# Attention's output projection: weight splits with a lead of 10, lo parts on POOL, chunks at 0.75 a half step

## The chip, the cores and the metric

The kernel runs on one core of a Trainium2 chip. A core has five engines that run side by side and wait for one another through semaphores: PE (TensorE, matrix products), DVE (VectorE) and ACT (ScalarE) for elementwise work and reductions, POOL (GpSimd) for elementwise work, and SP (SyncE), which here issues all DMAs. Each engine takes its instructions strictly in the order in which they stand. The metric is the device time of one launch in microseconds (us); less is better.

## What is computed

Two layers of a diffusion backbone over 256 latent tokens and 256 context tokens of width 1024. Layer 0 is a half-step SwiGLU FFN, a 2-D neighbourhood attention with 16 heads, and a second FFN; layer 1 has a short convolution in attention's place. Every sub-layer ends in a residual and a layer norm. All is float32. The part around the change, cut from the reference:

```python
bias = rpb[:, dy_idx[None, None, :, None], dx_b].reshape(N_HEADS, ncb, NA_QC, nk)
s_win = jnp.einsum('bjqhd,bjkhd->bhjqk', q_r, k_blk).astype(jnp.float32) * scale
s_win = jnp.where(mask, s_win + bias.astype(jnp.float32)[None], -jnp.inf)
s_ctx = jnp.einsum('bjqhd,bchd->bhjqc', q_r, k_c).astype(jnp.float32) * scale
p = jax.nn.softmax(jnp.concatenate([s_win, s_ctx], axis=-1), axis=-1).astype(v.dtype)
...
y_lat = jnp.moveaxis(o, 0, 1).reshape(B, S, D) @ w_out
...
x = post_norm_update(x, y_lat, m[:, 5], 1.0, ln_g[i, 1], ln_b[i, 1])
```

## The kernel before

Each float32 product is made of three products of a rounded type: an operand is split into a hi part (ACT copies it to the rounded type) and a lo part (the rest, a subtraction on DVE), and PE adds hi x hi, hi x lo and lo x hi (`mmu`, lines 156 to 159). For weights, `wunit` does it: it loads a raw block of 128x1024 by DMA (tile wor for the output projection), makes the hi part woh in two ACT instructions of 128x512 and the lo part wol in two DVE instructions of 128x512. Pools hold four raw blocks and five hi and lo blocks each; a load waits until the lo part of the block four units before has been made.

PE's order is the program's order, as it is written (`manual_schedule`). On the other engines a planner orders the instructions by priority; `high_priority(offset=n)` puts what stands inside it earlier by n places. The weight splits have an offset of 40 from the first FFN on, softmax's steps 40 and 70.

Attention has 32 half steps, one for a head and 128 queries. At each even step `scores` makes the scores S of a pair of heads (six matmuls), DVE adds the bias tile and takes the maximum, ACT takes the exponential and scales it (tile pr). The bias is loaded by four DMAs a pair, and POOL adds the window's mask to it (line 730). Two half steps later `probs_T` transposes the probabilities (PT, four matmuls) and splits them into pT hi (ACT) and lo (DVE); a step after that, for a head whose two query halves are there, `values` makes the eight matmuls o, whose halves are added (osum) and split (oT). The banks in PSUM are few: two for transposes, three for S and one half of the projection, three for o and the other half.

Between these steps stands a filler: at first the key, value and query projections, in the last eight half steps and behind them the output projection, `last_filler`. It goes by chunks: one chunk is one step of `out_gemm`, one weight unit for one bank, six matmuls of 128x512. There are eight units (pairs of K tiles for two halves of the columns) and sixteen chunks. The list `rate` says how many chunks stand at each half step; nine of them may stand among the softmax steps, the other seven behind them, since they need the last heads. Pairs of scores are numbered 0 to 15, chunks 1 to 16, units 1 to 8 in order of use.

Of the kernel before, what the change touches and what calls it, by code (L numbers as in the profile page):

```python
# [9 lines left out]
F32 = mybir.dt.float32  # L10
F32R = mybir.dt.float32r
AF = mybir.ActivationFunctionType
ALU = mybir.AluOpType
# [17 lines left out]
WB = (4, 5, 5)  # L31
PB = {"mm": 3, "at": 3, "tp": 2}
W_EARLY = 40
ADA_LATE = 20
LN_EARLY = 60
LEAD = 5
# [5 lines left out]
R0 = 2.4  # L42
R1 = 2.9
R2 = 1.9
R3 = 1.0
LN_LAG = (5, 5)
LT_LAG = (5, 5)
F0_LAG = (5, 5, 6, 7)
# [16 lines left out]
def backbone_kernel(  # L65
# [6 lines left out]
    nc = tc.nc  # L72
# [9 lines left out]

    uid = [0]
    w_early = [0]
    ext = [1, 0]
    ada_late = [0]

    def nm(s):
        uid[0] += 1
        return f"{s}_{uid[0]}"  # L90

    def act(dt=F32, s="a"):
        return ap.tile([P, 512], dt, tag="act", name=nm(s))
# [51 lines left out]
    def set_background(gen, rate):  # L145
        background[:] = [gen, rate, 0.0]
# [15 lines left out]
    def wunit(srcs, kn, s):  # L162

        raw = wp.tile([P, UN], F32, tag="wr", bufs=WB[0], name=nm(s + "r"))
        ext[1] += 1
        if ext[0] and ext[1] % (5 + ext[0]) in (E0 if ext[0] == 1 else E2):
            hi = hp.tile([P, UN], F32R, tag="whx", bufs=ext[0], name=nm(s + "h"))
            lo = hp.tile([P, UN], F32R, tag="wlx", bufs=ext[0], name=nm(s + "l"))
        else:
            hi = wp.tile([P, UN], F32R, tag="wh", bufs=WB[1], name=nm(s + "h"))  # L170
            lo = wp.tile([P, UN], F32R, tag="wl", bufs=WB[2], name=nm(s + "l"))
        rv, hv, lv = (t[:, :kn * 512].rearrange("p (a b) -> p a b", a=kn) for t in (raw, hi, lo))
        with tc.high_priority(offset=w_early[0]):
            for src, c in srcs:
                sync.dma_start(rv[:, :, c:c + src.shape[2]], src)
            m = kn * 512
            for a in range(0, m, m // W_HI):
                nc.scalar.activation(hi[:, a:a + m // W_HI], raw[:, a:a + m // W_HI], AF.Copy)  # L178
            for a in range(0, m, m // W_LO):
                b = a + m // W_LO  # L180
                nc.vector.tensor_tensor(out=lo[:, a:b], in0=raw[:, a:b], in1=hi[:, a:b].bitcast(F32), op=ALU.subtract)  # L181
        return hv, lv

    def wrows(w, r0, n, c0, s):
        src = w[r0:r0 + n * P, c0:c0 + 512].rearrange("(k p) n -> p k n", p=P)
        return wunit([(src, 0)], n, s)

    def wpair(w, u, c0, c1, s):
        if c1 == c0 + 256:
            return wrows(w, u * UK * P, UK, c0, s)  # L190
        src = w[u * UK * P:(u + 1) * UK * P, :].rearrange("(k p) n -> p k n", p=P)
        return wunit([(src[:, :, c0:c0 + 256], 0), (src[:, :, c1:c1 + 256], 256)], UK, s)
# [79 lines left out]
    def stream(*groups):  # L272
        for g in groups:
            yield from ada(g)
# [54 lines left out]
    def modulated(z, mv, rs, GB, lag):  # L329

        for h in range(2):
            nc.vector.tensor_scalar(z[h], z[h], mv[:, 0:1], rs, op0=ALU.subtract, op1=ALU.mult)

        def rest():
            G, B = GB.get()
            res = []
            for h in range(2):
                ps = tpb("hT")
                for k in range(4):
                    nc.tensor.transpose(ps[:, k * P:(k + 1) * P], z[h][:, k * P:(k + 1) * P], ident)  # L340
                t = sp.tile([P, 512], F32, tag="s2", bufs=S2, name=nm("h"))
                with tc.high_priority(offset=LN_EARLY):
                    hi, lo = act(F32R, "hTh"), act(F32R, "hTl")
                    for k in range(4):
                        s, c = slice(k * P, (k + 1) * P), slice(4 * h + k, 4 * h + k + 1)
                        nc.scalar.activation(t[:, s], ps[:, s], AF.Identity, bias=B[:, c], scale=G[:, c])
                    split(t, hi, lo)
                res.append((hi, lo))
            return res

        return Late(lag, rest)
# [29 lines left out]
    def run(gen):  # L381
        for _ in gen:
            pass
# [37 lines left out]
    def order_late(nu):  # L421

        e = nu - 1
        banks = ((0, 0), (0, 1), (1, 0))
        o = [(t, n, u) for t, n in banks for u in range(e - 1)]
        o += [(t, n, u) for u in (e - 1, e) for t, n in banks]
        return o + [(1, 1, u) for u in range(nu)]
# [47 lines left out]
    def start_step(k0, n):  # L475
# [31 lines left out]
        def mod(k, px):  # L507
            t = sp.tile([P, 512], F32, tag="s2", bufs=S2, name=nm("h"))
            hi, lo = act(F32R, "h0h"), act(F32R, "h0l")
            with tc.high_priority(offset=W_EARLY):  # L510
                for v in range(2):
# [62 lines left out]
    sync.dma_start(rope, rope_tab.rearrange("(t p) a b -> p t a b", p=P))  # L574
    w_early[0] = W_EARLY
    set_background(stream([(0, 2, 0), (0, 2, 1)], [(0, 3, 0), (0, 3, 1)], [(0, 4, 0), (0, 4, 1)],
# [5 lines left out]
    for fh, (p0, p1) in enumerate(parts):  # L582
# [16 lines left out]
        if fh == 0:  # L599
# [5 lines left out]
            background[1] = 0.4  # L605
            ada_late[0] = ADA_LATE

# [29 lines left out]
    def sub_end(w, lhs, nk, l, i, gm, wgt, nxt, s, order):  # L637


        gate = mod_rows(l, gm, "gate")  # L640
        lnr = None if nxt else ln_rows(l, i)
        GB = fold_cols(nxt[0], 0, nxt[1], (l, i)) if nxt else None
        st, hTs = {}, [None, None]

        def evac(t, n, bank, *c):
            if n == 0:
                st[t] = stat_tile(2 if nxt or t == 0 else 3)
            part = nxt is None and t == n == 1
            cs = slice(*(c or (0, 512)))
            residual(bank, xt[t][n][:, cs], gate[n][:, cs], wgt, None if c else ALPHA,  # L650
                     None if part and not c else st[t][:, n + (c[0] // 256 if c else 0)])
            if n == 1 and (not part or c and c[1] == 512):
                mv, rs = finish_stats(st[t])
                if nxt:
                    hTs[t] = modulated(xt[t], mv, rs, GB, (LN_LAG if nk > KC else LT_LAG)[t])
                else:
                    for h in range(2):
                        nc.vector.scalar_tensor_tensor(out=xt[t][h], in0=xt[t][h], scalar=mv[:, 0:1], in1=lnr[0][h],
                                                       op0=ALU.subtract, op1=ALU.mult)
                    for h in range(2):  # L660
                        nc.vector.scalar_tensor_tensor(out=xt[t][h], in0=xt[t][h], scalar=rs, in1=lnr[1][h],
                                                       op0=ALU.mult, op1=ALU.add)
                        sync.dma_start(out[0, t * P:(t + 1) * P, h * 512:(h + 1) * 512], xt[t][h])

        return out_gemm(w, lhs, nk, order, evac, s), hTs, (lambda: new_x(l, i))

    def lhs_T(tl):
        def f(k, t):
            s = (k % 2) * 256 + t * P
            g = tl[k // 2]  # L670
            hi, lo = g.get() if isinstance(g, Late) else g
            return hi[:, s:s + P], lo[:, s:s + P]
        return f
# [197 lines left out]
    def filler():  # L871
        yield from kv_quarter(1, KV)
        yield from kv_quarter(2, KV)
        yield from q_half(1, Q)
        yield from kv_quarter(3, KV)

    def last_filler():
        with tc.issue_after(bias_dma[-1].ins):
            for t in range(2):
                for h in range(2):  # L880
                    xt[t][h] = act(F32, "x")
                    sync.dma_start(xt[t][h], xscr[t * P:(t + 1) * P, h * 512:(h + 1) * 512])
            gen, nh, lt = sub_end(na_w_out[0], lhs_T(oT), KC, 0, 1, 5, 1.0, (0, 6), "wo", order_late(KU))
        box.extend([nh, lt])
        yield from gen

    box = []
    fill = filler()
    rate = [R0] * 8 + [R1] * 8 + [R2] * 8 + [R3] * 12
    credit = 0.0  # L890
    steps = [(h + i, qt) for h in range(0, NH, 2) for qt in range(2) for i in range(2)]
    prs = {}
# [37 lines left out]
                values(steps[j][0])  # L930
    run(fill)
    run(fin)
    phase.__exit__(None, None, None)
    hTs, later = box
    phase = tc.tile_pool(name="ph2", bufs=1)
# [127 lines left out]
```

## Time and profile before

| | us |
|---|---|
| median of 3 runs | 1286.15 |
| lowest, highest | 1283.31, 1291.49 |
| the profiled execution's own time | 1289.17 |
| its span | 1287.4 |

The second half of attention, on which the change works, runs from about 543 to 602 us of the span: S of pairs 10 to 15, the last transposes of the keys kT, chunks 1 to 16. Before it PE works on the projections, behind it follows the second FFN of layer 0. A matmul of 128x512 starts 0.23 us after the one before it, and its own length of 0.39 us overlaps the next. In the timeline's rows, the brackets hold the idle time of the engine ahead of an instruction and what ended it. In the views of waits, the numbers are the total, the count and the longest.

### The profile page before, as it was taken

The page shows a single profiled execution, that of the slowest core. Times are in us where ns is not written, and L with a number is a line of the kernel's source. Part 1 is how long each engine was busy: PE and PEld are TensorE (multiplying, and loading weights), DVE is VectorE, ACT ScalarE, POOL GpSimd, SP SyncE. Part 2 cuts the span into 40 slices and gives each one's busy share as a digit, 9 for nine tenths or more (in the row PEclk, how much of TensorE's full clock was granted, in tenths as well). Part 3 has the DMA queues.
Part 4 walks back from the last instruction along what each step waited for, and adds up shares of the span by engine and source line. Part 5 has one row for each costly group of instructions (what it writes and reads, how often), then busy time and mean ns, then how long its engine had stood idle before and what let it go on. Part 6 is the DMA issues. An engine that isn't in the chain of part 4 may idle for free.

```text
span 1287.4 us, 17193 instructions
## 1 busy us (share of the span) xinstructions
PE 1257.7 (98%) x5890; PEld 1007.0 (78%) x5890; DVE 955.1 (74%) x1683; ACT 591.2 (46%) x1148; POOL 42.0 (3%) x71
## 2 busy tenths in 40 slices
PE   7999999999999999988999999999999999999997
PEld 4787778788778877766887787887787877788886
DVE  3699877485658777788998787757778788855545
ACT  2432132413236456686555435654435645655431
POOL 0000000000001111110000000000000000000000
PEclk9999999999999999999999999999999999999999
DMA  9977569484622744464999887666887764666641
GB/s 284 299 231 243 181 193 297 131 297 146 198 78 76 215 91 92 90 147 149 305 331 328 295 294 262 215 215 225 289 287 241 215 211 147 210 217 185 231 155 51
DMA packets 202712, 268.59 MB, mean 209 GB/s; under 512 B 30026, under 2 KB 149298, under 8 KB 202624
## 3 DMA queue, kind: packets, MB, share of 16 engines
q1 hardware_dynamic: 202624, 267.49, 65.9%
q8 instruction: 46, 0.75, 0.2%
q14 instruction: 42, 0.34, 0.1%
HBM read 265.27 MB, written 2.17 MB: 208 GB/s over the span
## 4 chain that ended last, share of the span: by engine, by line
PE 78%; DVE 8%; DMA 8%; ACT 3%; issue 2%; SPq 1%; POOL 0%; DVEq 0%; ACTq 0%
PE w L156 13%; PE w L157 13%; PE w L159 13%; PE f L541 6%; PE f L542 6%; PE f L543 6%; DMA ar<-in_ada_w_dram 5%; DMA w1r<-in_ffn_w_in_dram 2%; PE wkv L156 2%; PE wkv L157 2%; PE wkv L159 2%; PE wc L156 2%; PE wc L157 2%; PE wc L159 2%; DVE w1l L181 2%
## 5 line engine op out<-in xcount | busy, mean ns | idle before, releaser
L178 ACT ACTIVATE w1h<-w1r 128x512 fp32r<-128x512 f32 x352 | 203.3, 626 | 185.0 <-PE w L159 75.4
L181 DVE TENSOR_TENSOR w1l<-w1r,w1h 128x512 fp32r<-128x512 f32 x352 | 227.6, 684 | 66.5 <-ACT w1h L178 64.3
L156 PE MATMUL w<-w1h,hTh 128*128 128x512 f32 x528 | 211.6, 401 | 3.8 <-ACT hTh L105 3.7
L247 DVE SCALAR_TENSOR_TENSOR acc<-ar,cst,acc 128x512 f32<-128x512 f32 x266 | 187.2, 745 | 34.8 <-DMA ar<-in_ada_w_dram 34.8
L157 PE MATMUL w<-w1l,hTh 128*128 128x512 f32 x528 | 207.7, 393 | 0.0
L156 PE MATMUL w<-w2h,gh 128*128 128x512 f32 (+1 forms) x446 | 175.4, 394 | 0.0
L157 PE MATMUL w<-w2l,gh 128*128 128x512 f32 (+1 forms) x446 | 173.7, 390 | 0.3 <-DVE w2l L181 0.3
L178 ACT ACTIVATE w2h<-w2r 128x512 fp32r<-128x512 f32 x176 | 101.5, 624 | 140.9 <-PE w L159 131.6
L159 PE MATMUL w<-w1h,hTl 128*128 128x512 f32 x528 | 163.9, 392 | 0.6 <-DVE hTl L106 0.6
L181 DVE TENSOR_TENSOR w2l<-w2r,w2h 128x512 fp32r<-128x512 f32 x176 | 114.0, 686 | 43.5 <-ACT w2h L178 42.3
L541 PE MATMUL f<-h0h,w1h 128*128 128x512 f32 x352 | 139.8, 397 | 0.4 <-ACT w1h L178 0.4
L542 PE MATMUL f<-h0h,w1l 128*128 128x512 f32 x352 | 138.4, 393 | 0.0
L543 PE MATMUL f<-h0l,w1h 128*128 128x512 f32 x352 | 138.3, 393 | 0.0
L159 PE MATMUL w<-w2h,gl 128*128 128x512 f32 (+1 forms) x446 | 136.3, 387 | 0.0
L156 PEld LDWEIGHTS w<-w1h,hTh 128*128 128x128 f32 x528 | 99.5, 188 | 28.2 <-ACT hTh L105 5.5
L159 PEld LDWEIGHTS w<-w1h,hTl 128*128 128x128 f32 x528 | 99.5, 189 | 24.1 <-DVE hTl L106 1.4
L157 PEld LDWEIGHTS w<-w1l,hTh 128*128 128x128 f32 x528 | 99.6, 189 | 20.4 <-DVE w1l L181 0.3
L156 PEld LDWEIGHTS w<-w2h,gh 128*128 128x128 f32 x446 | 83.7, 188 | 21.7 <-issue 1.7
L157 PEld LDWEIGHTS w<-w2l,gh 128*128 128x128 f32 x446 | 83.8, 188 | 18.6 <-DVE w2l L181 1.3
L159 PEld LDWEIGHTS w<-w2h,gl 128*128 128x128 f32 x446 | 83.3, 188 | 18.7
L541 PEld LDWEIGHTS f<-h0h,w1h 128*128 128x128 f32 x352 | 66.6, 189 | 18.4 <-issue 3.7
L543 PEld LDWEIGHTS f<-h0l,w1h 128*128 128x128 f32 x352 | 66.5, 189 | 14.7 <-DVE h0l L519 0.3
(178 smaller groups left out, 1702.5 us busy)
## 6 DMA issues: line engine op xcount, KB each, us to landing
w1r<-in_ffn_w_in_dram SPq DMA_DIRECT2D x352, 256.0 KB
ar<-in_ada_w_dram SPq DMA_DIRECT2D x128, 512.0 KB
w2r<-in_ffn_w_out_dram SPq DMA_DIRECT2D x88, 512.0 KB
ar<-in_ada_w_dram SPq DMA_DIRECT2D x32, 256.0 KB
wkvr<-in_na_w_qkv_dram SPq DMA_DIRECT2D x32, 256.0 KB
wcr<-in_sc_w_in_dram SPq DMA_DIRECT2D x32, 256.0 KB
wqr<-in_na_w_qkv_dram SPq DMA_DIRECT2D x8, 512.0 KB
bias<-in_na_rpb_dram SPq DMA_DIRECT2D x64, 64.0 KB
```

What stands on the lines that cost most here:

```text
L156: nc.tensor.matmul(ps, lh, rh, start=first and i == 0, stop=False)
L157: nc.tensor.matmul(ps, lh, rl, start=False, stop=False)
L159: nc.tensor.matmul(ps, ll, rh, start=False, stop=last and i == n - 1)
L178: nc.scalar.activation(hi[:, a:a + m // W_HI], raw[:, a:a + m // W_HI], AF.Copy)
L181: nc.vector.tensor_tensor(out=lo[:, a:b], in0=raw[:, a:b], in1=hi[:, a:b].bitcast(F32), op=ALU.subtract)
L247: nc.vector.scalar_tensor_tensor(out=a, in0=src, scalar=sc, in1=a, op0=ALU.mult, op1=ALU.add)
L541: nc.tensor.matmul(ps, lh, hT0[k][0], start=(k == 0), stop=False)
L542: nc.tensor.matmul(ps, ll, hT0[k][0], start=False, stop=False)
L543: nc.tensor.matmul(ps, lh, hT0[k][1], start=False, stop=(k == KC - 1))
```

## The change

While the output projection of attention is made (`calm`), a unit is split with an offset of 10 instead of 40. Its hi part is one ACT instruction of 128x1024, and its lo parts are two POOL instructions of 128x512 instead of two on DVE. Its load keeps the offset of 40. Through `rate`, half steps 24 to 31 take 0.75 chunks each instead of 1.0; the last four keep 1.0. No arithmetic changes.

```diff
+CALM = 10
+R4 = 0.75
...
         with tc.high_priority(offset=w_early[0]):
             for src, c in srcs:
                 sync.dma_start(rv[:, :, c:c + src.shape[2]], src)
-            m = kn * 512
+        m = kn * 512
+        if calm[0]:
+            with tc.high_priority(offset=CALM):
+                nc.scalar.activation(hi[:, :m], raw[:, :m], AF.Copy)
+                for a in range(0, m, 512):
+                    nc.gpsimd.tensor_tensor(out=lo[:, a:a + 512], in0=raw[:, a:a + 512],
+                                            in1=hi[:, a:a + 512].bitcast(F32), op=ALU.subtract)
+            return hv, lv
+        with tc.high_priority(offset=w_early[0]):
             for a in range(0, m, m // W_HI):
...
     def last_filler():
+        calm[0] = True
...
-    rate = [R0] * 8 + [R1] * 8 + [R2] * 8 + [R3] * 12
+    rate = [R0] * 8 + [R1] * 8 + [R2] * 8 + [R4] * 8 + [R3] * 4
...
     run(fin)
+    calm[0] = False
```

On PE, behind the scores of pair 13 (S_939; PT is a transpose of the probabilities, o a product with the values, wo a chunk), there stood before:

```order
L814 MATMUL S_939_5169<-kTh_907_5053,qTl_821_4643 128x512
L156 MATMUL wo_949_5206<-woh_947_5199,oT_724_4188 128x512
L157 MATMUL wo_949_5206<-wol_948_5200,oT_724_4188 128x512
L159 MATMUL wo_949_5206<-woh_947_5199,oT_725_4189 128x512 x2
L836 MATMUL PT_952_5215<-ident_75,pr_915_5077 128x128 x4
L848 MATMUL o_953_5222<-pT_903_5039,v_708_4110 128x256
```

There stands now:

```order
L825 MATMUL S_939_5167<-kTh_907_5053,qTl_821_4643 128x512
L847 MATMUL PT_948_5198<-ident_75,pr_915_5077 128x128 x4
L859 MATMUL o_949_5205<-pT_903_5039,v_708_4110 128x256
L860 MATMUL o_949_5205<-pT_904_5040,v_757_4365 128x256
L159 MATMUL wo_953_5225<-woh_951_5219,oT_724_4188 128x512
L160 MATMUL wo_953_5225<-wol_952_5220,oT_724_4188 128x512
```

The chunk no longer stands between S and PT but behind o; behind the scores of pair 15 it is the same.

On PE, at the end of softmax, from the last chunk before the last transposes to chunk 10 (wo on woh_1002), there stood before:

```order
L159 MATMUL wo_968_5288<-woh_982_5357,oT_902_5036 128x512 x2
L836 MATMUL PT_996_5423<-ident_75,pr_976_5338 128x128 x4
L836 MATMUL PT_997_5430<-ident_75,pr_978_5345 128x128 x4
L848 MATMUL o_998_5437<-pT_984_5370,v_830_4682 128x256
L848 MATMUL o_1000_5449<-pT_993_5408,v_830_4682 128x256
L156 MATMUL wo_930_5121<-woh_1002_5463,oT_988_5390 128x512
```

There stands now:

```order
L162 MATMUL wo_930_5120<-woh_991_5386,oT_902_5036 128x512 x2
L847 MATMUL PT_993_5398<-ident_75,pr_976_5328 128x128 x4
L162 MATMUL wo_953_5225<-woh_995_5406,oT_902_5036 128x512 x2
L847 MATMUL PT_997_5418<-ident_75,pr_978_5335 128x128 x4
L859 MATMUL o_998_5425<-pT_979_5339,v_830_4682 128x256
L162 MATMUL wo_969_5291<-woh_991_5386,oT_902_5036 128x512 x2
L859 MATMUL o_1000_5443<-pT_985_5369,v_830_4682 128x256
L159 MATMUL wo_930_5120<-woh_1002_5457,oT_983_5359 128x512
```

Of each chunk and each o one row is shown. One chunk has come between the last two transposes PT, and one between the last two o.

On POOL, in the middle of the second half (bias_881 and 882 are pair 11's bias, 895 and 896 pair 12's, 918 pair 13's), there stood before:

```order
L730 TENSOR_TENSOR bias_881_4940<-bias_881_4940,wmask_99 128x256
L730 TENSOR_TENSOR bias_882_4944<-bias_882_4944,wmask_99 128x256
L730 TENSOR_TENSOR bias_895_5007<-bias_895_5007,wmask_99 128x256
L730 TENSOR_TENSOR bias_896_5011<-bias_896_5011,wmask_99 128x256
L730 TENSOR_TENSOR bias_918_5088<-bias_918_5088,wmask_99 128x256
```

There stands now:

```order
L741 TENSOR_TENSOR bias_881_4940<-bias_881_4940,wmask_99 128x256
L184 TENSOR_TENSOR wol_934_5136<-wor_932_5134,woh_933_5135 128x512
L741 TENSOR_TENSOR bias_882_4944<-bias_882_4944,wmask_99 128x256
L184 TENSOR_TENSOR wol_952_5220<-wor_950_5218,woh_951_5219 128x512 x2
L184 TENSOR_TENSOR wol_967_5273<-wor_965_5271,woh_966_5272 128x512 x2
L741 TENSOR_TENSOR bias_895_5007<-bias_895_5007,wmask_99 128x256
L184 TENSOR_TENSOR wol_992_5387<-wor_990_5385,woh_991_5386 128x512 x2
L741 TENSOR_TENSOR bias_896_5011<-bias_896_5011,wmask_99 128x256
L741 TENSOR_TENSOR bias_918_5088<-bias_918_5088,wmask_99 128x256
```

The second lo part of wol_934 stands between bias_882 and wol_952 as well. The lo parts of units 2 to 5 now stand among the biases of pairs 11 and 12; those of unit 1 stand ahead of pair 9's, those of units 6 to 8 behind pair 15's.

On ACT the hi part of unit 5 now stands ahead of both scalings of pair 10, where the first half of it stood behind both; the hi parts of units 6 and 7 stand ahead of the exponentials or scalings of pair 15, and that of unit 8 stands between the last two osum copies. On SP the load of unit 5 is now issued ahead of pair 9's bias and that of unit 8 ahead of pair 13's, where they stood behind pair 9's and behind the loads of the layer norm's rows. In the FFNs some weight splits and sums of the adaLN rows (w1l, w2l, acc) change places on DVE, and so do a few of their loads on SP.

More of the change, by code (lines that the diff above doesn't have):

```diff
@@ L84, in backbone_kernel @@
     w_early = [0]
+    calm = [False]
     ext = [1, 0]
```

## The prediction

> **What bounds the kernel now.** I read the page first: its busy times and the chain of waits.
>
> ```profile
> PE 1257.7 (98%) x5890; PEld 1007.0 (78%) x5890; DVE 955.1 (74%) x1683; ACT 591.2 (46%) x1148; POOL 42.0 (3%) x71
> PE 78%; DVE 8%; DMA 8%; ACT 3%; issue 2%; SPq 1%; POOL 0%; DVEq 0%; ACTq 0%
> ```
>
> TensorE (PE) sets the time. Over the whole span it lacks 1287.4 - 1257.7 = 29.7 us of work, and a change that leaves its 5,890 matmuls alone can win only from that. POOL is idle 97% of the time. Next I took the stretches of the attention stage and of the first FFN behind it (columns: span, then busy time and count of PE, PEld, DVE, ACT, POOL, then the granted clock, DMA share, GB/s).
>
> ```profile
> 540.00:560.00 20.00, 16.74 (x97) 12.40 (x96) 17.43 (x38) 18.58 (x41) 3.52 (x4) 0.94 0.56 94
> 560.00:580.00 20.00, 19.50 (x114) 15.40 (x113) 15.67 (x35) 15.42 (x33) 4.94 (x6) 0.97 0.61 160
> 580.00:600.00 20.00, 16.87 (x89) 13.23 (x88) 15.25 (x33) 11.72 (x25) 1.61 (x3) 1.00 0.27 80
> 620.00:640.00 20.00, 20.00 (x94) 16.41 (x93) 17.69 (x31) 8.58 (x17) 0.00 (x0) 1.00 0.94 299
> ```
>
> From 540 to 600 us PE lacks 3.3, 0.5 and 3.1 us; from 620 on it lacks nothing. So the second half of attention is the place. Last, who PE waits for there (total, times, longest):
>
> ```profile
> PE kT L773 <- DVE pT L106: 2.0, 2, 1.5
> PE o L849 <- DVE pT L106: 1.5, 3, 0.6
> PE o L848 <- DVE osum L855: 0.9, 1, 0.9
> PE wo L156 <- ACT oT L105: 0.9, 1, 0.9
> PE o L848 <- ACT pT L105: 0.7, 1, 0.7
> PE PT L836 <- DVE pT L106: 0.5, 1, 0.5
> ```
>
> All are softmax steps on ACT and DVE that PE has caught up with, 6.5 us together. At the start of a matmul the loss is a little larger than the idle time, since the pipeline drains.
>
> **The change, part by part.**
>
> *Two projection chunks move* (a chunk is six matmuls on one weight unit). Each leaves the place behind the scores of pair 13 or pair 15, and all chunks slide back by one, so that one more stands before the last transpose PT and one between the last two value products o. The gaps that these fill:
>
> ```profile
> 582.40 0.48 PE L156 MATMUL wo<-woh,oT 128*128 128x512 f32 x1
> ...
> 583.89 0.60 PE L836 MATMUL PT<-ident,pr 128*128 128x128 f32 x4
> 585.03 0.66 PE L836 MATMUL PT<-ident,pr 128*128 128x128 f32 x4 [0.54 <-DVE pT L106]
> 585.44 0.36 PE L848 MATMUL o<-pT,v 128*128 128x256 f32 x1
> 586.23 0.39 PE L849 MATMUL o<-pT,v 128*128 128x256 f32 x1 [0.42 <-DVE pT L106]
> ...
> 587.04 0.28 PE L849 MATMUL o<-pT,v 128*128 128x256 f32 x1
> 588.24 0.38 PE L848 MATMUL o<-pT,v 128*128 128x256 f32 x1 [0.92 <-DVE osum L855]
> ...
> 590.83 0.50 PE L156 MATMUL wo<-woh,oT 128*128 128x512 f32 x1 [0.90 <-ACT oT L105]
> ```
>
> A chunk lasts 583.89 - 582.40 = 1.49 us. Unstalled, a PT is followed after about 0.4 us (585.03 to 585.44), and the o matmuls start 0.1 to 0.2 us apart. So the gaps cost 1.14 - 0.4 = 0.7, 0.79 - 0.2 = 0.6 and 1.20 - 0.1 = 1.1 us, 2.4 us in all, and each chunk is longer than what it covers. Gain 2.4 us (0 to 2.4). The last gap (0.90) stays: chunk 10 needs the last heads.
>
> What loses its cover where the chunks leave:
>
> ```profile
> 564.54 0.50 PE L814 MATMUL S<-kTh,qTh 64*128 64x512 f32 x2
> 565.44 0.50 PE L156 MATMUL wo<-woh,oT 128*128 128x512 f32 x1
> 566.94 0.60 PE L836 MATMUL PT<-ident,pr 128*128 128x128 f32 x4
> ...
> 577.78 0.50 PE L156 MATMUL wo<-woh,oT 128*128 128x512 f32 x1
> 564.19 0.71 ACT L824 ACTIVATE pr<-pr,mx 128x512 f32<-128x512 f32 x1
> 576.29 0.73 ACT L824 ACTIVATE pr<-pr,mx 128x512 f32<-128x512 f32 x1
> ```
>
> Without its chunk the first PT could go at 565.44; its probabilities are ready at 564.90. The second could go at 577.78; its input is ready at 577.02. Both are covered, by 0.5 and 0.8 us: cost nothing (up to 0.7 us each, if softmax runs later). But the scores of pairs 14 and 15 now come 1.5 us sooner after those of pair 13, and their bias may not be there:
>
> ```profile
> 571.90 1.43 POOL L730 TENSOR_TENSOR bias<-bias,wmask 128x256 f32<-128x256 f32 x2 [9.87 <-DVE oT L106]
> ```
>
> Pair 14's bias was ready only at 573.33. I charge 0.1 us (0 to 1.5), because the last unit's load, which stood ahead of it in SP's queue, is now issued before pair 13's bias.
>
> *The lo parts leave DVE.* Sixteen subtractions, about 0.67 us each, leave a queue in which the softmax steps stand behind them:
>
> ```profile
> L181 DVE TENSOR_TENSOR wol<-wor,woh x32: 661/684/851, 518.6 to 1066.6; 128x512 fp32r<-128x512 f32 x32
> 550.51 0.66 DVE L181 TENSOR_TENSOR wol<-wor,woh 128x512 fp32r<-128x512 f32 x1
> 554.35 0.66 PE L773 MATMUL kT<-ident,kr 128*128 128x128 f32 x4 [0.41 <-DVE pT L106]
> 556.55 0.66 PE L773 MATMUL kT<-ident,kr 128*128 128x128 f32 x4 [1.55 <-DVE pT L106]
> ```
>
> That is 10.7 us of DVE time, but most of it beside PE's work. On PE's path lie the waits of 549 to 556.5 us: 0.7 + 0.6 + 0.4 + 1.5 = 3.2 us. Followed by hand in the new order, the first two shrink to about 0.8 together, since ACT does the hi parts in one pass and DVE's pT comes at once. The last two fall to about 0.5. But a hi part of 128x1024 now stands ahead of both scalings of pair 10, and the next PT waits for that by 0.9 us. 3.2 - 2.2 = 1.0 us gain (a loss of 0.5 to a gain of 2.0).
>
> *The lo parts on POOL.* The trace has no 128x512 subtraction there. The nearest rows:
>
> ```profile
> L730 POOL TENSOR_TENSOR bias<-bias,wmask x32: 724/737/1192, 419.4 to 576.0; 128x256 f32<-128x256 f32 x32
> 597.31 0.52 POOL L325 TENSOR_TENSOR rs<-mv,lnc 128x1 f32<-128x1 f32 x1 [20.41 <-DVE mv L323]
> ```
>
> Below: 0.52 fixed plus twice (0.737 - 0.52) is 0.95 us. Above: twice 0.737 is 1.47, and twice the slowest, 1.192, is 2.38. I take 1.3 us, near the doubled bias row, which is the same two-input form. The first lo of unit 2 follows its hi part:
>
> ```profile
> 543.29 0.69 DVE L181 TENSOR_TENSOR wol<-wor,woh 128x512 fp32r<-128x512 f32 x1 [0.35 <-ACT woh L178]
> 552.62 3.23 SPq L726 DMA_DIRECT2D bias<-in_na_rpb_dram  x4
> ```
>
> In one piece the hi part ends some 0.35 us later, at 543.65. Before pair 13's bias can be issued, SP must issue the loads of units 6 to 8, which wait for six lo parts and one bias: 543.65 + 6 x 1.3 + 0.74 = 552.2, plus about 0.4 for the load's own issue: 552.6, as before. Cost nothing at 1.3 us.
>
> [...]
>
> *POOL beside DVE.* One wait may grow:
>
> ```profile
> 545.57 0.96 DVE L106 TENSOR_TENSOR oT<-osum,oT 128x256 fp32r<-128x256 f32 x1
> 556.42 0.41 DVE L106 TENSOR_TENSOR oT<-osum,oT 128x256 fp32r<-128x256 f32 x1
> ```
>
> The same instruction took 0.55 us longer while POOL worked on a bias. At the end, the last oT now meets the last unit's lo parts, and ACT's last hi part stands ahead of the osum before it: 0.4 us on PE's path (0 to 1.5).
>
> [...]
>
> *Clock.* After the kT wait the matmuls run slow:
>
> ```profile
> 558.56 0.79 PE L156 MATMUL wo<-woh,oT 128*128 128x512 f32 x1
> 561.23 0.60 PE L836 MATMUL PT<-ident,pr 128*128 128x128 f32 x4
> ```
>
> That chunk took 2.67 us instead of 1.49, in the stretch with clock 0.94. PE still idles some 2 us there, in smaller pieces; I leave it as it is: 0 (a gain of 1.7 to a loss of 1.2).
>
> *Elsewhere* the planner swaps weight splits and adaLN sums on DVE in the FFNs. PE waits for neither there: 0, plus or minus 1 us.
>
> **Sum.** 2.4 + 1.0 - 0.1 - 0.4 = 2.9 us, against the profiled execution's 1289.17 (span 1287.4 and 1.8 around it): 1286.3. That execution lies 3.0 above the median of 1286.15, so for the median: 1283.2.
>
> **The rivals.**
>
> POOL becomes the pace. Each 0.1 us above 1.3 delays pair 13's bias, and pair 14's behind it, by 0.6 us. About 1 us of that is slack, so the gain is gone at (2.9 + 1) / 6 = 0.65 more, from 2.0 us an instruction on. At 2.38 it is 6.5 - 1 - 2.9 = 2.6 us slower: 1288.8. For it: the contended bias rows, and the SP queue. [...] To be over 1% slower it takes (12.9 + 3.9) / 6 = 2.8 us more, above 4 us an instruction, for which no row speaks; but none shows POOL writing this type either. Chance 0.25, of which 0.08 over 1%.
>
> The gain is given back: softmax's own chain (bias, maximum, exponential, scaling) is what PE waits for at the end wherever the chunks stand. Pair 14's late bias speaks for it, the covers of 0.5 and 0.8 us against. 1286.2. Chance 0.17.
>
> The clock stays up too: another 1.7 us, 1281.5. For it, smaller idle pieces; against, their sum hardly shrinks. Chance 0.13.
>
> The forecast as it stands: 0.45, its own range 1281.5 to 1285.
>
> **How the numbers follow.** 1283.2 is the likeliest case. From 1279.5 (clock and the full gain of DVE's part) to 1289.5 (POOL at 2.4 us) all is taken in but the last 0.08 and the edges. A change of 1%, 12.9 us, is about what a measurement of this kernel can tell from none. Faster by that: all waits of the stage and the clock give 6.5 + 1.7 us, which isn't enough, 0.02. Slower: 0.08. Within: 0.90.
>
> **What would show it.** The waits on DVE pT and on osum behind 583 us gone, the one on oT left; kT's 1.5 us halved; POOL's lo parts near 1.3 us; the first w1 matmul about 3 us earlier; the same PE work. Wrong would be: lo parts above 2 us, PE waiting for POOL's wol, or S waiting for a bias.

## The result, and the profile after

| | before | after |
|---|---|---|
| median, us (22 runs each) | 1287.25 | 1291.43 |
| lowest to highest | 1283.07 to 1291.49 | 1288.47 to 1294.85 |
| span of the profiled execution | 1287.4 | 1289.2 |

The ratio is 1.0041, with a 95% interval of 1.0032 to 1.0049: the change costs 0.41%, some 5.3 us (the two medians lie 4.2 us apart). The forecast was 1283.2 (1279.5 to 1289.5): wrong in sign and out of range. First the busy times of after, from the page.

```profile
PE 1256.5 (97%) x5890; PEld 1005.9 (78%) x5890; DVE 947.1 (73%) x1667; ACT 591.1 (46%) x1140; POOL 62.2 (5%) x87
```

PE's work is the same, and 16 instructions have gone from DVE to POOL. Next who PE waits for in attention's second half (total, times, longest).

```profile
PE PT L847 <- DVE pT L109: 3.1, 1, 3.1
PE o L860 <- DVE pT L109: 2.1, 2, 1.1
PE o L859 <- ACT pT L108: 1.2, 2, 0.7
PE kT L784 <- DVE pT L109: 1.1, 1, 1.1
PE wo L159 <- ACT oT L108: 1.1, 1, 1.1
PE wo L162 <- DVE oT L109: 0.6, 1, 0.6
```

The wait for osum is gone and the kT waits have shrunk from 2.0 to 1.1 us, but a single wait of 3.1 us is new. The stretches of after (columns as in the prediction: span, PE, PEld, DVE, ACT, POOL, granted clock, DMA share, GB/s) say where it lies:

```profile
540.00:560.00 20.00, 16.98 (x102) 12.74 (x102) 12.90 (x30) 18.19 (x38) 12.83 (x12) 1.00 0.54 110
560.00:580.00 20.00, 14.85 (x80) 10.96 (x78) 11.44 (x26) 11.93 (x28) 4.51 (x7) 0.87 0.67 142
580.00:600.00 20.00, 18.25 (x94) 13.98 (x95) 12.70 (x26) 10.94 (x21) 7.58 (x6) 0.96 0.28 79
```

Before, PE worked 19.50 us of the middle stretch at clock 0.97; now 14.85 at 0.87. Four places on PE cut the stage into stretches: the first scores of pairs 10, 13 and 15, the start of the last o, and the first transpose hT behind the projection. PE's timeline in before (pair 13's scores at 564.54 and the last o at 588.24 stand in the prediction):

```profile
544.86 0.50 PE L814 MATMUL S<-kTh,qTh 64*128 64x512 f32 x2
576.71 0.50 PE L814 MATMUL S<-kTh,qTh 64*128 64x512 f32 x2
599.09 0.66 PE L340 MATMUL hT<-ident,x 128*128 128x128 f32 x4 [0.26 <-DVE x L332]
```

And in after, with the waits between them:

```profile
544.10 0.49 PE L825 MATMUL S<-kTh,qTh 64*128 64x512 f32 x2
562.50 0.39 PE L860 MATMUL o<-pT,v 128*128 128x256 f32 x1 [1.12 <-DVE pT L109]
563.52 0.50 PE L825 MATMUL S<-kTh,qTh 64*128 64x512 f32 x2
575.54 1.08 PE L847 MATMUL PT<-ident,pr 128*128 128x128 f32 x4 [3.09 <-DVE pT L109]
577.34 0.58 PE L859 MATMUL o<-pT,v 128*128 128x256 f32 x1 [0.72 <-ACT pT L108]
579.86 0.79 PE L825 MATMUL S<-kTh,qTh 64*128 64x512 f32 x2
591.67 0.28 PE L859 MATMUL o<-pT,v 128*128 128x256 f32 x1
594.33 0.50 PE L159 MATMUL wo<-woh,oT 128*128 128x512 f32 x1 [1.08 <-ACT oT L108]
603.48 0.66 PE L351 MATMUL hT<-ident,x 128*128 128x128 f32 x4 [0.26 <-DVE x L343]
```

Between the scores of pairs 13 and 15 there stands one chunk less than before, and one more behind pair 15, so 1.49 us is put back into the first of these stretches and taken out of the second. Lost (+) or won (-) against before, in us:

| stretch | before | after | with the chunk set right |
|---|---|---|---|
| pair 10 to pair 13 | 19.68 | 19.42 | -0.26 |
| pair 13 to pair 15 | 12.17 | 16.34 | +5.66 |
| pair 15 to the last o | 11.53 | 11.81 | -1.21 |
| the last o to hT | 10.85 | 11.81 | +0.96 |
| together | 54.23 | 59.38 | +5.15 |

The 5.15 us are near the 5.3 of the ratio, but they belong to these two executions, and outside the stage they differ the other way: the one of after took 0.76 us less up to pair 10 and 2.6 us less behind hT, which is why the two spans lie only 1.8 us apart. In those two parts the profiled execution of before is the slowest of all that were profiled, so that difference isn't put down to the change. More than all of the 5.15 us is lost between pairs 13 and 15. What came late there shows on DVE and POOL in after:

```profile
574.37 0.43 DVE L829 TENSOR_TENSOR S<-S,bias 128x256 f32<-128x256 f32 x1 [4.92 <-POOL bias L741]
574.71 0.68 DVE L109 TENSOR_TENSOR pT<-PT,pT 128x512 fp32r<-128x512 f32 x1
...
573.62 1.40 POOL L741 TENSOR_TENSOR bias<-bias,wmask 128x256 f32<-128x256 f32 x2 [8.00 <-DMA bias<-in_na_rpb_dram]
```

DVE sits 4.92 us before pair 14's bias, the split pT of a finished transpose stands behind it in DVE's order, and PE waits for that split's bank. SP's rows tell why the bias is late; after:

```profile
553.89 0.55 SPq L178 DMA_DIRECT2D wor<-in_na_w_out_dram  x1
554.53 4.47 SPq L737 DMA_DIRECT2D bias<-in_na_rpb_dram  x4
...
561.21 3.90 SPq L894 DMA_DIRECT2D x<-xscr  x4
...
566.15 5.65 SPq L737 DMA_DIRECT2D bias<-in_na_rpb_dram  x8
```

And before, where pair 13's four loads (552.62, in the prediction) took 3.23 us:

```profile
559.94 0.39 SPq L175 DMA_DIRECT2D wor<-in_na_w_out_dram  x1
560.43 1.83 SPq L882 DMA_DIRECT2D x<-xscr  x4
...
563.30 6.38 SPq L726 DMA_DIRECT2D bias<-in_na_rpb_dram  x8
```

The last unit's load (wor at 553.89) now stands ahead of pair 13's bias. Pair 13's bias is issued 1.9 us later, its issues take 1.2 us longer, those of x 2.1 us longer, and pair 14's bias goes out at 566.15 instead of 563.30. It can be masked some 8 us after that (8.6 us in before, 7.5 in after).

### The profile page after: what moved, and what is told of

Same layout as the page of the kernel before. It is cut to its first block, busy times and chain, and to the rows that moved or that the text cites. A ratio compares the mean times of both kernels' runs of the same rounds, so it can differ in the third digit from the quotient of the medians.

```text
span 1289.2 us, 17201 instructions
## 1 busy us (share of the span) xinstructions
PE 1256.5 (97%) x5890; PEld 1005.9 (78%) x5890; DVE 947.1 (73%) x1667; ACT 591.1 (46%) x1140; POOL 62.2 (5%) x87
## 4 chain that ended last, share of the span: by engine, by line
PE 89%; DVE 4%; DMA 3%; ACT 2%; issue 1%; POOL 1%; SPq 0%; DVEq 0%; POOLq 0%; ACTq 0%
PE w L159 17%; PE w L160 17%; PE w L162 17%; PE f L552 6%; PE f L553 6%; PE f L554 6%; PE wkv L159 2%; PE wc L159 2%; PE wc L160 2%; PE wkv L160 2%; PE wkv L162 2%; PE wc L162 2%; DMA bias<-in_na_rpb_dram 1%; DMA w1r<-in_ffn_w_in_dram 1%; PE gT L411 1%; PE ada L276 1%
```

## Experiments

The theory going in, "late bias": the change lets pair 14's scores come sooner and its bias later, and what PE loses is that wait. The rivals: the splits alone (POOL's lo parts set the pace), the chunks' places alone, the clock.

**rate_alone**: only the chunks move.

```diff
     def last_filler():
-        calm[0] = True
+        calm[0] = False
```

> The change with the weight splits as before (two hi pieces, lo parts on DVE, offset 40); only the two chunks move. Times against 1287.2 us for the kernel before. 'Late bias' (what PE loses is the wait for pair 14's bias, which had no slack before): pair 14's scores come 1.5 us sooner, their bias as late as before (POOL from about 571.9 us), so 1.5 us of new waiting on DVE pT between the scores of pairs 14 and 15, and the two chunks fill 1 to 2.4 us at the end: 1285.5 to 1287.8 us. 'The splits alone do it' (POOL's lo parts hold up what stands behind them): no loss here, only the 2.4 us of the filled gaps: 1284.9. 'The chunks alone do it' (the place behind the scores is uncovered): the whole loss is here, 1290 or more.

1286.42 us; ratio 0.9998 (0.9984 to 1.0011). No loss, so "the chunks alone" falls. But no new wait either: SP and POOL of this run show the bias as early as it is wanted.

```profile
562.36 7.01 SPq L737 DMA_DIRECT2D bias<-in_na_rpb_dram  x8
...
570.18 1.43 POOL L741 TENSOR_TENSOR bias<-bias,wmask 128x256 f32<-128x256 f32 x2 [8.83 <-DMA bias<-in_na_rpb_dram]
```

My expectation that it would come as late as before was wrong; it was issued 0.9 us sooner.

**calm_alone**: only the splits change.

```diff
-    rate = [R0] * 8 + [R1] * 8 + [R2] * 8 + [R4] * 8 + [R3] * 4
+    rate = [R0] * 8 + [R1] * 8 + [R2] * 8 + [R3] * 12
```

> The change with 1.0 chunks a half step as before; only the splits change. 'Late bias': DVE's relief brings pair 14's scores 1.0 us sooner (569.3), the loads behind POOL's lo parts bring the bias 1.7 us later (POOL at 573.6): 2.7 us of new waiting before the scores of pair 15, less the 1.0 us won, and 1 us lost at the end where the last oT meets POOL's lo parts: 1289 to 1291 us. 'The splits alone do it': 1291 or more, with PE's waits on POOL wol. 'The chunks alone do it': 1286.2, the 1.0 us of DVE won.

1290.96 us (six runs); 1.0041 (1.0027 to 1.0055): the whole loss. PE waits for no wol; it waits for the split behind the bias (its waits, then SP's timeline), which is issued as late as in after:

```profile
PE o L860 <- DVE pT L109: 5.6, 4, 3.3
```

```profile
566.26 5.73 SPq L737 DMA_DIRECT2D bias<-in_na_rpb_dram  x8
```

**after_bias14**: after, with pair 14's bias loaded at pair 12's step.

```diff
-            if i % 2 == 0 and i + 2 < len(steps):
-                bias_pair(*steps[i + 2])
+            if i % 2 == 0 and i + 2 < len(steps) and i not in (26,):
+                [bias_pair(*steps[j]) for j in ((i + 2, 28) if i == 24 else (i + 2,))]
```

> The changed kernel with pair 14's bias loaded and masked one pair earlier, so that its four loads stand on SP ahead of the reloads of x and gate (six transfers of 256 KB). 'Late bias': POOL's mask for pair 14 starts at 568 to 570 us instead of 573.6 and the wait of 3.1 us on DVE pT is gone; next late is pair 15's bias, whose loads stay behind x and gate (0 to 2.5 us lost there): 1286.5 to 1289 us. Any other theory (POOL's pace, chunk places, the clock by itself): nothing that it names is changed, 1291.4 within 1 us.

1290.71 us; 1.0031 (1.0016 to 1.0046). The place is right and the price wrong: by the time alone this run is where I had put every other theory (1291.4 within 1 us), and only the trace tells them apart. POOL's second mask of pair 14 starts at 570.68, and the wait of 3.1 us is gone; pair 15's bias, behind the six reloads, is masked only from 578.58 on, and the same wait stands one pair later:

```profile
570.68 0.74 POOL L741 TENSOR_TENSOR bias<-bias,wmask 128x256 f32<-128x256 f32 x1 [2.74 <-DMA bias<-in_na_rpb_dram]
578.58 0.73 POOL L741 TENSOR_TENSOR bias<-bias,wmask 128x256 f32<-128x256 f32 x1 [7.15 <-DMA bias<-in_na_rpb_dram]
...
582.11 0.24 PE L308 MATMUL mcT<-ident,mrow 32*128 32x32 f32 x1 [2.77 <-DVE pT L109]
```

**after_bias1415**: the same for pairs 14 and 15, in buffers of their own.

```diff
-            bt = hp.tile([P, 4, 64], F32, tag="bias", bufs=4, name=nm("bias"))
+            bt = hp.tile([P, 256], F32, tag="kr", bufs=8, name=nm("bias")).rearrange("p (a b) -> p a b", a=4) if h == 14 else hp.tile([P, 4, 64], F32, tag="bias", bufs=4, name=nm("bias"))
...
+            if i % 2 == 0 and i + 2 < len(steps) and i not in (26, 28,):
+                [bias_pair(*steps[j]) for j in ((i + 2, 28, 30) if i == 24 else (i + 2,))]
```

> The changed kernel with the biases of pairs 14 and 15 loaded and masked at pair 12's step, into buffers of their own (the idle ones of the keys' transposes); x, gate and the last two weight units are loaded behind them. 'Late bias': both waits are gone, the granted clock from 560 to 580 us is 0.95 or more instead of 0.87, the scores of pair 15 start before 576 us instead of at 579.9: 1285 to 1287 us. 'Clock by itself': the clock is low there again, and 2 us or more stay lost. 'POOL's pace': 1291 within 1 us, PE waits for wol or a bias.

1284.35 us; 0.9980 (0.9967 to 0.9992), faster than both kernels. Its middle stretch, and pair 15's scores on PE:

```profile
560.00:580.00 20.00, 19.74 (x119) 15.19 (x118) 16.50 (x39) 18.24 (x39) 7.82 (x10) 1.00 0.66 192
```

```profile
573.11 0.50 PE L825 MATMUL S<-kTh,qTh 64*128 64x512 f32 x2
```

With the bias in time the loss is gone, and the clock of that stretch is 1.00 (0.87 in after): the drop went with the wait, and is no loss of its own here.

**before_bias1415**: the control, the same edit on before.

> The kernel before with the biases of pairs 14 and 15 loaded early into buffers of their own, as in after_bias1415: a control. 'Late bias': before, PE lost only 0.5 us to that bias (the wait on DVE pT at 575.7), so 0 to 1 us faster than before: 1286 to 1287. 'The early loads win something else' (that is, after_bias1415 says nothing of the change): 5 us or more faster here as well, 1282 or less.

1287.31 us; 1.0000 (0.9987 to 1.0014). Early biases win nothing where they weren't late. The wait of 0.5 us that I had put down to the bias (o at 575.69 in before) stands here too, so the bias was not its cause:

```profile
575.92 0.39 PE L849 MATMUL o<-pT,v 128*128 128x256 f32 x1 [0.51 <-DVE pT L106]
```

**rate_bias1415** and **calm_bias1415**: the same edit on rate_alone and on calm_alone.

> The two chunks moved, the splits as before, the biases of pairs 14 and 15 early: the counterpart of after_bias1415 without POOL's lo parts and the lead of 10. In rate_alone PE hardly waits for the bias (pair 14's was ready at 571.6), so 'late bias' gives 1285.5 to 1286.5 us here and leaves the splits' own move, with the bias in time, 1 to 2 us of gain in after_bias1415 (1284.35). If the splits' move has no worth of its own: 1284.4 here too.

> The splits of the change and the early biases of pairs 14 and 15, with 1.0 chunks a half step as before: what the splits' move is worth when the bias is in time. 'Late bias': without the chunks' move 1.0 to 1.8 us are won up to the scores of pair 13, 1 us is lost at the last oT, and the gaps at the end stay open: 1285.5 to 1287 us against 1286.8 for before, some 2 us over after_bias1415. 'The splits cost of themselves': 1288.5 or more.

1284.93 us, 0.9983 (0.9969 to 0.9996), and 1286.38 us, 0.9992 (0.9978 to 1.0006). With the bias in time the chunks win 0.1 to 0.2%. The splits on top of them win 0.03% (0.9980 against 0.9983), or 0.09% by the repeat below: these runs can't tell that from nothing. Nor do they show a cost of their own.

**calm_dve**: after, with the lo parts on DVE.

```diff
-                    nc.gpsimd.tensor_tensor(out=lo[:, a:a + 512], in0=raw[:, a:a + 512],
+                    nc.vector.tensor_tensor(out=lo[:, a:a + 512], in0=raw[:, a:a + 512],
```

> The change with the lo parts on DVE, everything else as in it (hi in one piece, offset of 10, 0.75 chunks). 'POOL's chain' (a unit's load waits for a lo part four units before; on POOL at 1.3 us each, behind one another and behind bias masks, these come late, and with them the biases behind the loads in SP's queue): pair 14's bias is issued at 563 to 564 us as without the splits' move, 1285.5 to 1288 us. 'The lead' (10 instead of 40, one hi piece of 1.06 us): the loads come as late as in the changed kernel (bias issued at 566), 1290 to 1292.

1287.50 us; 1.0004 (0.9994 to 1.0014). The bias is issued at 563.06, as "POOL's chain" said, so the lead of 10 isn't the cause. But with the lo parts on DVE the planner also put the last unit's load behind pair 15's bias; the next kernel moves that load alone.

**after_wor8**: after, with one load moved.

```diff
-        with tc.high_priority(offset=w_early[0]):
+        with (tc.issue_after(bias_dma[-1].ins) if calm[0] and (calm.append(0) or len(calm)) - 1 in (8,) else tc.high_priority(offset=w_early[0])):
             for src, c in srcs:
```

> The changed kernel with one load moved: the last weight unit's stands behind pair 15's bias in SP's queue, not ahead of pair 13's. 'POOL's chain': pair 13's bias is issued some 1.5 us sooner (it no longer waits for POOL's lo parts of unit 4, done at 553.4), pair 14's 1 to 2.5 us sooner, PE's wait of 3.1 us shrinks by as much: 1288.5 to 1290.5 us. If that load is not what holds the queue: 1291.4 within 0.7 us.

1287.69 us; 1.0008 (0.9997 to 1.0018). One load of 512 KB accounts for 3.3 of the 4.1 parts in a thousand, more than I expected: pair 14's bias is issued 3.75 us sooner.

```profile
562.40 5.79 SPq L737 DMA_DIRECT2D bias<-in_na_rpb_dram  x8
...
570.05 1.43 POOL L741 TENSOR_TENSOR bias<-bias,wmask 128x256 f32<-128x256 f32 x2 [8.30 <-DMA bias<-in_na_rpb_dram]
```

POOL's lo parts are unchanged in number, length and order, so it isn't their pace. What is left fits the sooner scores: pair 14's start at 567.51 instead of 570.26, 2.75 us ahead of before, and its bias is masked 1.85 ahead. Pair 15's second mask is late as well here, at 578.14 (575.97 in before).

**bias1415_late8** and **after_bias1415_again**: the tail term. ACT's last oT is kept, and the hi part of the last unit queued behind it.

```diff
-            with tc.high_priority(offset=CALM):
+            with tc.issue_after(calm[1].ins) if (calm.append(0) or len(calm)) - 2 == 8 else tc.high_priority(offset=CALM):
...
-            split(osum[0], *(z[:, cs] for z in oT[h // 4]))
+            calm[1:] = [split(osum[0], *(z[:, cs] for z in oT[h // 4]))] + calm[2:]
```

> after_bias1415 with the last weight unit's hi part behind the last oT on ACT, so that its lo parts on POOL come behind the last oT on DVE. 'POOL shuts DVE out': the last oT on DVE takes 0.42 us again instead of 1.53, ACT's osum no longer waits for the hi part (1.06 us); of the 1.0 us that the change lost there 0.8 to 1.2 comes back, 0.8 to 1.2 us less than after_bias1415_again. If PE waits for the last unit instead (its lo parts are ready only at about 589.5, its first use is some 7 us after the last oT), or if that oT is long for another reason: no gain.

> after_bias1415 once more, on the chip of these runs: 0.998 of the kernel before within 0.001, as the first time.

1284.38 us, 0.9976 (0.9963 to 0.9990), against 1284.39, 0.9974 (0.9962 to 0.9987): no gain. DVE's last oT in after_bias1415, then in bias1415_late8, and there PE's new waits:

```profile
586.92 1.53 DVE L109 TENSOR_TENSOR oT<-osum,oT 128x256 fp32r<-128x256 f32 x1 [0.48 <-ACT oT L108]
```

```profile
586.55 0.42 DVE L109 TENSOR_TENSOR oT<-osum,oT 128x256 fp32r<-128x256 f32 x1 [0.48 <-ACT oT L108]
...
588.87 0.50 PE L160 MATMUL wo<-wol,oT 128*128 128x512 f32 x1 [0.85 <-POOL wol L184]
590.54 0.50 PE L160 MATMUL wo<-wol,oT 128*128 128x512 f32 x1 [0.94 <-POOL wol L184]
```

DVE's last oT is short again, 0.42 us ahead of POOL's lo parts (they start at 587.54) against 1.53 beside them (585.66 to 588.17), but the last unit is used 2.3 us after that oT, not some 7 as I had assumed, and PE waits 1.8 us for it instead.

The stretches of all the kernels, lost (+) or won (-) against before in us, as in the table above, and the ratio. Each is one execution: the last stretches of calm_alone, after_bias14 and after_bias1415_again hold a drop of the clock as well (0.78, 0.91 and 0.91 from 580 to 600 us).

| kernel | 10 to 13 | 13 to 15 | 15 to last o | last o to hT | together | ratio |
|---|---|---|---|---|---|---|
| after | -0.26 | +5.66 | -1.21 | +0.96 | +5.15 | 1.0041 |
| rate_alone | -0.19 | +0.30 | -1.41 | +0.52 | -0.78 | 0.9998 |
| calm_alone | -0.38 | +2.87 | +1.67 | +2.43 | +6.59 | 1.0041 |
| calm_dve | +0.13 | +1.76 | -0.84 | +0.34 | +1.39 | 1.0004 |
| after_wor8 | -0.26 | +1.62 | -0.25 | +0.96 | +2.07 | 1.0008 |
| after_bias14 | +0.19 | -0.20 | +2.01 | +2.15 | +4.15 | 1.0031 |
| after_bias1415 | -1.27 | -0.29 | -1.86 | +0.97 | -2.45 | 0.9980 |
| after_bias1415_again | -1.25 | -0.30 | -1.85 | +2.16 | -1.24 | 0.9974 |
| bias1415_late8 | -1.19 | -0.30 | -1.84 | +1.86 | -1.47 | 0.9976 |
| calm_bias1415 | -1.24 | -0.46 | +0.54 | +0.02 | -1.14 | 0.9992 |
| rate_bias1415 | +1.41 | +0.42 | -2.06 | +0.53 | +0.30 | 0.9983 |
| before_bias1415 | +1.37 | -0.01 | +0.02 | +0.04 | +1.42 | 1.0000 |

Between pairs 13 and 15, every kernel with both biases early stays within 0.5 us of before. Between pairs 10 and 13 the clock tells: from 540 to 560 us it is 1.00 in after, calm_alone, after_bias14, after_bias1415 and after_wor8, with the lo parts on POOL, and 0.88 to 0.94 in all five executions with them on DVE (0.88 in before_bias1415 and rate_bias1415, which lose 1.4 us there). The other three with the lo parts on POOL show it by their matmuls: from 543 to 560 us no single one of 128x512 takes over 0.50 us, where before has two of 0.63 and one of 0.79. So with the lo parts on POOL the clock stayed up in this stretch; how much of that reaches the time of the whole kernel, the ratios can't tell.

## Why the prediction was wrong

Term by term, gains with a plus:

| term of the prediction | predicted | after | after_bias1415 |
|---|---|---|---|
| two chunks fill the gaps at the end | +2.4 | +1.21 | +1.86 |
| the lo parts leave DVE, with the clock of that stretch (0) | +1.0 | +0.26 | +1.27 |
| pair 14's bias | -0.1 | -5.66 | +0.29 |
| the last oT beside POOL | -0.4 | -0.96 | -0.97 |
| sum | +2.9 | -5.15 | +2.45 |

**The step that failed** is "I charge 0.1 us (0 to 1.5), because the last unit's load, which stood ahead of it in SP's queue, is now issued before pair 13's bias." Two things were wrong in it. The load had not left the queue; it had moved from just ahead of pair 14's bias to ahead of pair 13's, and everything behind it moved later (after_wor8). And the bound was too small by the prediction's own terms: pair 14's scores come 1.5 us sooner by the chunk and 1.0 by DVE's relief, and the bias was ready only at 573.33. DVE in before adds it at once, without a wait for it:

```profile
573.10 0.75 DVE L818 TENSOR_TENSOR S<-S,bias 128x256 f32<-128x256 f32 x2
```

One add takes 0.43 us (the row of 574.37 in after), so the second began at about 573.4, 0.1 us after its half of the bias was there. The prediction's "About 1 us of that is slack" had this wrong too. With no slack, every microsecond won ahead of that point turns into a wait at it. Supply 1.7 us later (573.62 against 571.90) and demand 2.5 us sooner make a hole of 4.2 us; the rows show 3.09 and 0.72 us of waiting, and most of the rest of the 5.66 is the half clock behind it (0.50 from 576 to 578 us, in the last section).

**The timing under it**: "552.6, as before" for pair 13's bias. The length was right, 1.29 us a lo part, but the chain began late: on POOL one of pair 11's masks stands ahead of the lo parts of unit 2 and one between them, as the listing of its order shows, and only the one between was counted. POOL in after:

```profile
544.32 0.74 POOL L741 TENSOR_TENSOR bias<-bias,wmask 128x256 f32<-128x256 f32 x1 [6.32 <-PE PT L847]
545.02 1.49 POOL L184 TENSOR_TENSOR wol<-wor,woh 128x512 fp32r<-128x512 f32 x1
546.46 0.73 POOL L741 TENSOR_TENSOR bias<-bias,wmask 128x256 f32<-128x256 f32 x1
547.15 6.24 POOL L184 TENSOR_TENSOR wol<-wor,woh 128x512 fp32r<-128x512 f32 x5
...
556.80 2.54 POOL L184 TENSOR_TENSOR wol<-wor,woh 128x512 fp32r<-128x512 f32 x2
559.46 0.73 POOL L741 TENSOR_TENSOR bias<-bias,wmask 128x256 f32<-128x256 f32 x1
```

The first lo part starts at 545.02, not at 543.65 (its hi part had ended at 542.93), and the sixth ends at 553.39. The last unit's load could go at once, at 553.89, and pair 13's bias at 554.53.

**DVE's relief** was sized too high. The waits of the two lists that lie between 549 and 556.5 us shrank from 3.2 to about 3.0 us (of after's list 2.1 + 1.2 + 1.1 + 0.5, without the 1.12 of 562.50 and the 0.72 of 577.34), not to 2.2. What else was won there is the clock: 1.00 from 540 to 560 us instead of 0.94. From pair 12's scores to the second chunk behind them PE took 2.98 us instead of 4.44, so most of the 1.7 us of the rival "the clock stays up too" came. And 1.12 us went into the wait of 562.50: pair 12's second mask stands behind two lo parts (556.80, 2.54 us), and DVE waited 1.84 us for it before its half of S. That POOL's order can hold up a mask I had weighed for pair 13 alone.

**The chunks**: the gaps they were to fill are gone, as predicted. Of 2.4 us 1.2 to 1.9 came. In after_bias1415 the missing 0.5 us stands at three transposes: two start 0.70 and 0.53 us after the last matmuls of the chunk ahead of them, where 0.46 was usual, and one is followed by its o after 0.58 us, not 0.35. In after the half clock takes another 0.7: from pair 15's scores to the first o behind them 2.14 us instead of 1.47.

**The last oT**: 0.96 us, within the bounds of 0 to 1.5 but over the value of 0.4. DVE's last oT took 1.53 us beside POOL's lo parts in after_bias1415 and 0.42 ahead of them in bias1415_late8. But POOL isn't all of the 0.96: rate_alone and rate_bias1415, whose lo parts are on DVE, lose 0.5 us in the same stretch (PE waits 1.5 us for ACT's oT instead of 0.9, and on DVE a lo part stands ahead of osum), and calm_bias1415, with the lo parts on POOL and the chunks in their old places, loses 0.02. So about half of it came with the chunks' move.

**The rivals**: POOL as the pace, by longer lo parts, was not it (1.29 us). "The gain is given back" named the right place, but took the gain as the most that could be lost there. What the text said would make it wrong, S waiting for a bias, is what happened.

**The numbers around it.** Of the 8.2 us between the forecast and the median, 1.1 lie in its base, three runs at 1286.15 where 22 give 1287.25. The lower end of its range doesn't follow from the two terms it names: 1.7 and 1.0 below 1283.2 is 1280.5. And a measurement tells more than the 1% it allowed for: the interval of the ratio is 0.17% wide.

Left open: how the last unit's load delays what stands behind it. Its own turn on SP is 0.64 us (553.89 to 554.53). More of the 3.75 us by which after_wor8 has pair 14's bias sooner is in slower issues: the last six bias loads ahead of x took 6.87 us in after and 5.07 in after_wor8, the four of x 3.90 and 1.78. Whether its bytes cause this, no kernel here shows.

## What to carry to other kernels

Before you count a gain ahead of a synchronisation point, read the arrival of each of its operands from the trace: an operand that is just in time turns everything won ahead of it into a wait. A load that moves forward in SP's queue can be paid for by every load it passes (one load moved back brought pair 14's bias forward by 3.75 us), so look at what stands behind its new place. The cure here was to bring the next thing that is late forward with the change: with both biases early the change is 0.2% faster than before (0.9980 and 0.9974; without the splits it is 0.9983), and half the cure (pair 14 alone) only moves the wait one pair on.

## What was not expected of the hardware

Some small loads take SP two to three times as long to issue as others just like them. In before the bias loads of this stage took 595 to 1225 ns each, in after up to 1742 (SP's loads of the tile bias, least, median, most):

```profile
L726 SPq DMA_DIRECT2D bias<-in_na_rpb_dram x19: 595/607/1225, 539.9 to 569.1; - x19
```

```profile
L737 SPq DMA_DIRECT2D bias<-in_na_rpb_dram x18: 595/604/1742, 539.9 to 571.2; - x18
```

The slow ones of after stand behind the 512 KB loads wor of 550.92 and 553.89 (the bias loads behind them took 2.40 us for two and 4.47 for four), but the two behind the wor of 548.45 took only 1.26, so a large load ahead is not the whole reason.

In the traces of before and after PE's clock falls from 1.00 to 0.50, not by degrees: in windows of 0.25 us up to 1280 us it is one or the other in all but four of before and two of after. In after it stood at 0.50 from 575.00 us, within the wait of 3.09 us, to 581.75 (the seventh number of after's stretches):

```profile
572.00:574.00 2.00, 0.45 (x2) 0.02 (x1) 0.00 (x0) 0.00 (x0) 0.39 (x1) 1.00 0.72 87
576.00:578.00 2.00, 1.20 (x4) 0.51 (x3) 1.77 (x5) 1.98 (x6) 0.73 (x1) 0.50 0.64 184
...
582.00:584.00 2.00, 2.00 (x16) 1.83 (x15) 1.96 (x5) 1.34 (x3) 1.91 (x2) 1.00 0.00 0
```

In before the clock fell 1.2 us behind a wait of 1.55 us (0.50 from 557.75 to 561.00), and in after_bias14 it did not fall at once after one of 2.77 (1.00 from 580 to 590), so the length of one wait doesn't foretell it. Nor does the kernel: in the repeat of after_bias1415 the matmuls of 128x512 between 588.11 and 591.09 us start 0.43 us apart and take 0.63 each (clock 0.91 from 580 to 600), and in the first execution, with the same waits up to there (1.08 and 0.60 us), they start 0.23 apart and take 0.39 (clock 1.00).
